# Turning the dilated queries by VectorE and DRAM instead of by TensorE, and a later place for the first pair's bias loads

## The chip, the cores and the metric

The kernel runs on one core of one Trainium2 chip. The metric is the device time of one execution in microseconds (us). Before the change it is 857.27 us, the median of three runs (856.55 to 859.91).

## The reference

Two encoder layers over 512 tokens of 1024 channels, 16 heads of 64. The first mixes tokens by dilated attention (three groups of dilation 1, 4 and 16, merged by their softmax denominators), the second by attention over a two-dimensional neighbourhood. The change lies in the first layer:

```python
def mixer_a(hn, w_in, w_out, q_gain, k_gain, t5_bias):
    proj = hn @ w_in                                  # 1024 x 10240
    qkv = proj[..., :n_qkv].reshape(b, s, 3, 3, N_HEADS, HEAD_DIM)
    gate = proj[..., n_qkv:]
    for g, (window, dilation) in enumerate(((128, 1), (512, 4), (2048, 16))):
        q = rms_norm(qkv[:, :, g, 0], q_gain[g])
        k = rms_norm(qkv[:, :, g, 1], k_gain[g])
        v = qkv[:, :, g, 2]
        reach = (window // 2) // dilation
        o, lse = dilated_group_attention(q, k, v, t5_bias[...], dilation, reach)
        ...                                           # softmax over a band, plus bias
    alpha = softmax(stack(lses)); y = sum(alpha * stack(outs))
    return (y * silu(gate)) @ w_out
```

All of it is float32. `setup_inputs` scales the gains and biases by about 8, so the precision is needed.

## The kernel before, in words

**Work and tiles.** Heads go in 8 pairs (`hc` 0 to 7). The normalised input lies as `hn_h` and `hn_l`, a high and a low part, and each weight block of 512 KB is loaded raw (`wraw`, eight slots, mostly on SyncE's queue, some added in by GpSimd's), cast by ScalarE to its high part `wh`, and its rest is made by VectorE or GpSimd as `wl`. A product is then three matmuls (high by high, low by high, high by low: the groups of three over `acc`). The products of a pair are mixed in the manner of Strassen (`mixed`), so that one pair's q, k, v and gate take 32 block jobs.

**Order.** A generator `main` emits the products and a generator `side` the attention of the pair before; `run` interleaves them by a model clock. `later_on(delay, f)` puts `f` at a later time of that clock, `yield "wait", key, delay` stays until a stamp is that old. The order so found is the program's order on TensorE (a manual schedule) and, under `held`, also on ScalarE, VectorE, GpSimd and SyncE; each engine then works its list off in that order. Nearly every operation of those engines is recorded at the line of one helper, L85; matmuls are L324, transposes on TensorE L328.

**Around the change.** When the products of a pair's queries are done, `normed("rawq")` squares, sums and scales the raw tiles (`rawq`, `rawk`: 4 row blocks of 128 tokens). `q_a` then turns tokens and channels by TensorE with an identity (`tp<-ident,rawq`, 4 transposes fill one PSUM bank): k0 and q0 of the undilated group first, then the queries of the two dilated groups, g = 0 and 1, each four transposes and one ScalarE copy into `q12` (in the profile `q<-tp`). `k_a` does the same for the dilated keys (`tp<-ident,rawk`, two groups, copied with the key gain as `k<-tp,gk`). After that `attn_a` makes the logits (`log`): per tile t two banks, one for each head, q0 by k0 as three products and then 32 small matmuls `log<-k,q` per head pair. `tp`, `log` and `o` share four PSUM banks, so the logits of tile t = 1 need the two banks that the copies of k set free.

The bias of the next pair's logits comes as six loads per pair (`e<-l_d`, `bias_a`) on SyncE's queue, the probabilities of the pair are rearranged by 16 moves `pt<-pt` there, and `weigh` multiplies them with v (`o<-pt,v`). `gt` is the gated output; `y_split` splits the outputs for the last product into `y_h` and `y_l`.

Of the kernel before, what the change touches and what calls it, by code (L numbers as in the profile page):

```python
# [13 lines left out]
F32 = mybir.dt.float32  # L14
# [8 lines left out]
P = 128  # L23
# [12 lines left out]
PB = 4  # L36
# [10 lines left out]
def tile_hybrid_encoder(  # L47
# [42 lines left out]
    @contextmanager  # L90
    def in_order():

        was, held[0] = held[0], True
        yield
        held[0] = was
# [3 lines left out]
    def sb(t, off, dims):  # L99
        return bass.AP(t.tensor, t.offset + off, [t.ap[0]] + dims)  # L100
# [54 lines left out]
    turn, pool = [0], [[2, 5]]  # L155
# [160 lines left out]
    clock = [0.0]  # L316
# [27 lines left out]
    def later_on(delay, job):  # L344

        timers.append((clock[0] + delay, job))
        timers.sort(key=lambda t: t[0])
# [92 lines left out]
    def transpose4(raw, c):  # L440
        tp = bank("tp")
        for i in range(4):
            transpose(tp[:, i * P : (i + 1) * P], raw[:, i, c : c + P])
        return tp
# [168 lines left out]
    def project_qk(n, ns, key, hc, guard, first=False, **kw):  # L613
# [22 lines left out]
            return  # L636
        normed(raw, ss, ns, key, hc)

    def normed(raw, ss, ns, key, hc):

        def go():
            with in_order() if hc == 0 and key != "raw" else nullcontext():
                head_norm(raw, ss, ns, key == "raw")
            st[key, hc] = raw
            stamp[key, hc] = clock[0]

        if (key, hc) == ("rawk", 0):
            later_on(4000, go)
        elif held[0]:
            later_on(2200, go)  # L650
        else:
            go()
# [107 lines left out]
    def q_a(hc):  # L760

        yield "wait", ("rawq", hc), (22000, 10500)[hc] if hc < 2 else 8000
        raw = st.pop(("rawq", hc))
        q0h = wk.tile([P, 512], F32R, tag="q0h", name="q0h", bufs=1)
        q0l = wk.tile([P, 512], F32R, tag="q0l", name="q0l", bufs=1)
        k0h = wk.tile([P, EXT], F32R, tag="k0h", name="k0h", bufs=1)
        k0l = wk.tile([P, EXT], F32R, tag="k0l", name="k0l", bufs=1)
        q12 = wk.tile([P, 2, 512], F32, tag="q12", name="q12", bufs=1)
        tp = bank("tp")
        for i in range(4):  # L770
            transpose(tp[:, i * P : i * P + P].rearrange("p (r j) -> p j r", j=4), raw[:, i, 3 * P :])
        act.activation(k0h[:, 64:EXT], tp, AF.Copy, scale=gk[:, 0:1])
        yield 1000
        vec.scalar_tensor_tensor(
            k0l[:, 64:EXT], tp, gk[:, 0:1], k0h[:, 64:EXT].bitcast(F32), op0=ALU.mult, op1=ALU.subtract
        )
        yield 400
        tp = transpose4(raw, 0)
        act.copy(q0h, tp)
        yield 1000  # L780
        vec.tensor_sub(q0l, tp, q0h.bitcast(F32))
        yield 400
        for g in range(2):
            act.copy(q12[:, g, :], transpose4(raw, P + P * g))
            yield
        stamp["q", hc] = 0
        st["q", hc] = q0h, q0l, q12, k0h, k0l

# [62 lines left out]
    def weighed(hc, os):  # L851
        gt, rest = st.pop(("gate", hc))
        for _ in rest:
            pass
        for j in range(4):
            g = by_class(gt)[:, :, j]
            vec.tensor_mul(g, g, os[j][:, :P].rearrange("p (t r) -> p t r", t=4))
        return gt
# [7 lines left out]
    def y_split(t, hc):  # L866
        src = t.rearrange("p (t ja x) -> p x ja t", t=4, ja=8)
        h, l = (u[:, hc, :].rearrange("p (x ja t) -> p x ja t", x=16, ja=8) for u in (st["y_h"], st["y_l"]))
        with in_order():
            act.copy(h, src)  # L870
            (vec if hc % 2 else pol).tensor_sub(l, src, h.bitcast(F32))
        stamp["ya", hc, "y"] = 0

    def bias_a(hc):
        e0 = wk.tile([P, 2, 256], F32, tag="e0", name="e0", bufs=1)
        e12 = wk.tile([P, 4, 224], F32, tag="e12", name="e12", bufs=1)
        for hd in range(2):
            h = 2 * hc + hd
            syn.dma_start(
                e0[:, hd, :],  # L880
                bass.AP(l0_d.tensor, l0_d.offset + h * 1600 + 127, [[400, 4], [-4, 32], [1, 256]]),
            )
            for g in range(2):
                syn.dma_start(
                    e12[:, 2 * hd + g, :],
                    bass.AP(l12_d.tensor, l12_d.offset + h * 512 + 256 * g + 31, [[0, 4], [-1, 32], [1, 224]]),
                )
        return e0, e12
# [49 lines left out]
    def attn_a(hc):  # L938
# [9 lines left out]
        def turn(hd, t, pr, n):  # L948

            dst = sb(pq, at(t, hd) + 256 * (4 - n), [[256, n], [1024, 4], [1, 32]])  # L950
            src = pr[:, 512 - P * n : 512]
            vec.transpose(dst, src.rearrange("p (i b k) -> p i b k", b=4, k=32))
# [12 lines left out]
        def scores(u):  # L965

            tiles = []
            for t in (2 * u, 2 * u + 1):
                cs, n = (64, 192) if t == 0 else (0, 192) if t == 3 else (0, 256)
                tiles.append((t, [bank("log") for _ in range(2)], cs, n))  # L970
            for t, lgs, cs, n in tiles:
                ks = slice(P * t + cs, P * t + cs + n)
                qs = slice(P * t, P * t + P)
                mm3_heads(
                    [lg[:, cs : cs + n] for lg in lgs],
                    lambda hs: q0h[hs, qs], lambda hs: q0l[hs, qs],
                    lambda hs: k0h[hs, ks], lambda hs: k0l[hs, ks], False,
                )
            for t, lgs, cs, n in tiles:
                for g in range(2):  # L980
                    for j in range(4):
                        c = P * t + 32 * j
                        for hd in range(2):
                            hs = slice(64 * hd, 64 * hd + 64)
                            matmul(
                                lgs[hd][32 * j : 32 * j + 32, 256 + P * g : 384 + P * g],
                                q12[hs, g, c : c + 32],
                                by_class(k12[hs, g, :])[:, :, j],
                                share=2,
                                start=False,  # L990
                                stop=(g == 1),
                            )
            return [(hd, t, lgs[hd], cs, n) for t, lgs, cs, n in tiles for hd in range(2)]
# [43 lines left out]
        def weigh():  # L1037
            os, v0 = [bank("o") for _ in range(4)], st.pop("v0")
            mms = []
            for g in range(2):  # L1040
                for b in range(4):
                    for j in range(4):
                        own = slice(32 * j, 32 * j + 32)
                        c, d = P * g, 1024 * b + 256 * (2 + g)
                        mms.append((
                            lambda hs, j=j: os[j][hs, :P],
                            lambda hs, own=own, b=b, c=c: v12[own, b, c + hs.start : c + hs.stop],
                            lambda hd, own=own, d=d: pq[own, d + at(0, hd) : d + at(0, hd) + P],
                        ))
            for i in range(4):  # L1050
                (ta, ia), (tb, ib) = ((i - 1, 1), (i, 0)) if i else ((0, 0), (3, 1))
                n, m = 32 * (tb - ta), 256 * (ib - ia) + 32 * (tb - ta)
                for a in range(4):
                    mms.append((
                        lambda hs, a=a, d=32 * ta, n=n: sb(os[a][hs], d, [[n, 2], [1, 32]]),
                        lambda hs, i=i: v0[:, i, hs],
                        lambda hd, d=run * a + 256 * ia + 32 * ta, m=m: sb(t0, d + 128 * hd, [[m, 2], [1, 32]]),
                    ))
            yield from side_by_side(mms, 4)
            return os  # L1060
# [48 lines left out]
        fill = bias_rows() if hc == 2 else None  # L1109
        yield from v_a(hc)  # L1110
        yield "wait", ("pt", hc), 2500
        st["e", hc + 1] = bias_a(hc + 1)
        yield "wait", ("pt", hc), (4500, 11500)[hc] if hc < 2 else 9000 if hc == NHC - 2 else 7500
        yield "wait", ("gate", hc), 4000
        gt = weighed(hc, (yield from weigh()))
        if hc < NHC - 2:
            send = lambda: tc.keep_in_program_order(syn.dma_start(y_d[:, hc, :], gt))
            later_on(3000, send)
            stamp["w", hc] = 0
            yield  # L1120
            if fill:
                later_on(1500, fill)
            yield 1500
            yield from q_a(hc + 1)
            return
# [391 lines left out]
```

## Time and profile before

| | |
|---|---|
| median of 3 runs | 857.27 us (856.55 to 859.91) |
| the profiled execution: own time, span | 857.42 us, 855.6 us |
| TensorE matmul busy | 833.8 us, 97% |
| VectorE, ScalarE, GpSimd busy | 636.0 us (74%), 508.8 us (59%), 294.5 us (34%) |
| mean granted clock of TensorE | 0.992 |
| moved from and to DRAM | 131.97 MB, mean 154 GB/s |

The profile records one execution. Its span lies 1.8 us below its own time, and its own time 0.15 us above the median, so a forecast made from this profile can be set against the median directly. Rows of a timeline give the start and the duration in us, the engine, the line, the operation with its tiles, the number of instructions taken together, and in brackets what an idle time before it waited for. TensorE's matmuls overlap, so that the distance between starts tells more than durations do.

### The profile page before, as it was taken

What the parts mean: (1) busy time and instruction counts of PE and PEld (TensorE: products, weight loads), DVE (VectorE), ACT (ScalarE), POOL (GpSimd) and SP (SyncE); (2) the same over time, 40 slices, a digit from 0 to 9 for tenths busy, and PEclk for the clock granted to TensorE, in tenths of its full rate; (3) what the DMA queues carried; (4) which work ended last, traced back from release to release, by engine and by line L of the source; (5) the groups of instructions that cost most, each with busy time, mean ns of one, the idle gap of its engine ahead of it and who ended that gap; (6) DMA issues with size and microseconds to landing.
All of it is one profiled execution on the core that took longest, in us unless ns stands there. A gap on an engine that the chain in (4) does not pass through costs nothing.

```text
span 855.6 us, 18127 instructions
## 1 busy us (share of the span) xinstructions
PE 833.8 (97%) x6611; PEld 689.7 (81%) x6611; DVE 636.0 (74%) x1654; ACT 508.8 (59%) x1066; POOL 294.5 (34%) x258
## 2 busy tenths in 40 slices
PE   8998989999999999999999999999999999999998
PEld 6876868878877878878878887789998898889786
DVE  7899895897897787786886865656578666776742
ACT  7566665755845846846847738545456654665440
POOL 5045442362453543443533512113123322322301
PEclk9999999999999999999999999999999999999999
DMA  9425755776576775776776554283264456534212
GB/s 339 137 59 136 205 130 140 135 176 189 133 183 191 156 189 168 162 174 180 152 181 179 117 184 142 75 300 113 80 193 142 124 170 183 162 131 127 84 50 99
DMA packets 56169, 131.97 MB, mean 154 GB/s; under 512 B 7184, under 2 KB 24528, under 8 KB 55952
## 3 DMA queue, kind: packets, MB, share of 16 engines
q1 hardware_dynamic: 49744, 108.78, 40.9%
q0 software_dynamic: 6048, 22.02, 15.3%
q8 instruction: 52, 0.85, 0.4%
q14 instruction: 37, 0.30, 0.1%
q10 hardware_dynamic: 288, 0.01, 0.0%
HBM read 111.73 MB, written 11.72 MB: 144 GB/s over the span
## 4 chain that ended last, share of the span: by engine, by line
PE 74%; DVE 9%; ACT 8%; DMA 4%; issue 3%; SPq 1%; POOL 1%; DVEq 0%; ACTq 0%
PE acc L324 61%; ACT p L85 5%; PE o L324 4%; PE log L324 4%; PE tp L328 3%; DMA wraw<-in_w 2%; DVE wl L85 2%; SPq L85 1%; ACT rawk L85 1%; ACT wh L85 1%; DVE na L85 1%; DVE rawq L85 1%; DVE p L85 1%; DVE gt L85 1%; DMA pt<-in_xt 1%
## 5 line engine op out<-in xcount | busy, mean ns | idle before, releaser
L85 POOL TENSOR_TENSOR wl<-wraw,wh 128x512 fp32r<-128x512 f32 (+1 forms) x153 | 197.6, 1292 | 426.8 <-PE acc L324 227.8
L85 ACT CAST wh<-wraw 128x512 fp32r<-128x512 f32 (+1 forms) x360 | 209.4, 593 | 196.6 <-PE acc L324 160.1
L85 DVE TENSOR_TENSOR wl<-wraw,wh 128x512 fp32r<-128x512 f32 (+1 forms) x207 | 160.2, 777 | 43.2 <-PE acc L324 34.3
L324 PE MATMUL acc<-wh,hn_h 128*128 128x384 f32 (+1 forms) x488 | 185.9, 381 | 2.9 <-DVE gt L85 1.7
L324 PE MATMUL acc<-wl,hn_h 128*128 128x384 f32 (+1 forms) x488 | 176.7, 362 | 1.4 <-DVE wl L85 1.4
L324 PE MATMUL acc<-wh,hn_l 128*128 128x384 f32 (+1 forms) x488 | 176.8, 362 | 0.0
L85 ACT ACTIVATE p<-p,mn 128x256 f32<-128x256 f32 (+2 forms) x248 | 137.5, 583 | 32.3 <-DVE mn L85 32.3
L324 PEld LDWEIGHTS acc<-wh,hn_h 128*128 128x128 f32 x488 | 91.8, 188 | 21.4 <-issue 6.8
L324 PEld LDWEIGHTS acc<-wl,hn_h 128*128 128x128 f32 x488 | 91.9, 188 | 9.8 <-DVE wl L85 2.5
L324 PEld LDWEIGHTS acc<-wh,hn_l 128*128 128x128 f32 x488 | 91.6, 188 | 9.6
L324 PE MATMUL acc<-wl,mix_h 128*128 128x512 f32 x224 | 87.9, 393 | 2.1 <-DVE wl L85 2.1
L324 PE MATMUL acc<-wh,mix_h 128*128 128x512 f32 x224 | 89.5, 400 | 0.0
L324 PE MATMUL acc<-wh,mix_l 128*128 128x512 f32 x224 | 87.8, 392 | 0.0
L324 PE MATMUL acc<-hn_h,wh 128*128 128x512 f32 x192 | 79.0, 411 | 0.3 <-ACT rawb L85 0.2
L324 PE MATMUL acc<-hn_h,wl 128*128 128x512 f32 x192 | 75.2, 391 | 0.0
L324 PE MATMUL acc<-hn_l,wh 128*128 128x512 f32 x192 | 74.9, 390 | 0.0
L85 DVE STREAM_TRANSPOSE pt<-p 128x512 f32<-128x512 f32 (+1 forms) x60 | 40.6, 687 | 23.7 <-ACT p L85 23.5
L85 DVE TENSOR_REDUCE ss<-sq 128x4 f32<-128x256 f32 (+1 forms) x96 | 46.1, 501 | 11.9 <-POOL sq L85 6.2
L324 PE MATMUL acc<-y_h,wh 128*128 128x512 f32 x128 | 52.3, 409 | 0.0
L324 PEld LDWEIGHTS acc<-wl,mix_h 128*128 128x128 f32 x224 | 42.4, 189 | 11.5 <-DVE wl L85 3.3
L324 PE MATMUL acc<-y_h,wl 128*128 128x512 f32 x128 | 50.5, 394 | 0.0
L324 PE MATMUL acc<-y_l,wh 128*128 128x512 f32 x128 | 50.4, 394 | 0.0
(149 smaller groups left out, 1373.0 us busy)
## 6 DMA issues: line engine op xcount, KB each, us to landing
wraw<-in_w SPq DMA_DIRECT2D x95, 512.0 KB
wraw<-in_w POOLq DMA_DIRECT2D x42, 512.0 KB, 6.9
wraw<-in_w SPq DMA_DIRECT2D x38, 384.0 KB
pt<-pt SPq DMA_DIRECT2D x112, 64.0 KB
td<-tr SPq DMA_DIRECT2D x24, 224.0 KB
pt<-td SPq DMA_DIRECT2D x24, 224.0 KB
e<-l_d SPq DMA_DIRECT2D x32, 112.0 KB
e<-l_d SPq DMA_DIRECT2D x16, 128.0 KB
```

The source lines that it names most:

```text
L85: m = f(*args, **kw)
L324: nc.tensor.matmul(o, l, r, **kw)
L328: nc.tensor.transpose(o, i, ident)
```

## The change

There are four parts.

1. For pairs 2 to 7 a new function `move_q` takes the dilated queries off TensorE. As soon as a pair's `rawq` blocks are scaled, VectorE turns them in 32x32 blocks (four instructions `qt<-rawq`), ScalarE's queue writes them to DRAM in two transfers (`qd<-qt`, 256 KB each) and reads them back in four (`q<-qd`, 128 KB each, in runs of 512 bytes). `q_a` then leaves out 8 transposes and 2 copies per pair and waits in the model clock for the last read.
2. `q12` has another order of columns. Pairs 0 and 1 keep TensorE's transposes but need four half copies where two whole ones were.
3. The rest `y_l` of pair 1 is made by GpSimd instead of VectorE.
4. `bias_a(1)`, the loads of the bias for the second pair, is emitted behind the first pair's `weigh` instead of ahead of it.

```diff
+    def move_q(raw, hc):
+        d = dr.tile([2, P, 512], F32, tag="qd", name="qd", bufs=2)
+        halves = []
+        def turn(i):
+            if i % 2 == 0:
+                halves.append(wk.tile([P, 512], F32, tag="p", name="qt", bufs=PB))
+            dst = sb(halves[-1], 32 * (i % 2), [[64, 2], [128, 4], [1, 32]])
+            vec.transpose(dst, raw[:, i, P : 3 * P].rearrange("p (g b k) -> p g b k", g=2, k=32))
+            if i % 2:
+                later_on(1500, partial(act.dma_start, d[i // 2], halves[-1]))
+        def read(b):
+            if b == 0:
+                st["q12", hc] = wk.tile([P, 1024], F32, tag="q12", name="q12", bufs=1)
+            dst = sb(st["q12", hc][32 * b : 32 * b + 32], 0, [[128, 8], [1, 128]])
+            src = bass.AP(d.tensor, d.offset + 128 * b, [[512, 32], [512 * 32, 8], [1, 128]])
+            act.dma_start(dst, src)
+            if b == 3:
+                stamp["q12", hc] = clock[0]
+        for i in range(4):
+            later_on(1600 + 1000 * i, partial(turn, i))
+            later_on(11500 + 800 * i, partial(read, i))
...
         def go():
+            if key == "rawq" and hc > 1:
+                move_q(raw, hc)
...
-        for g in range(2):
-            act.copy(q12[:, g, :], transpose4(raw, P + P * g))
+        for g in range(0 if moved else 2):
+            tp = transpose4(raw, P + P * g).rearrange("p (h t j r) -> p h t j r", h=2, t=2, j=4)
+            for h in range(2):
+                act.copy(sb(q12, 512 * h + 64 * g, [[32, 2], [128, 4], [1, 32]]), tp[:, h])
             yield
+        if moved:
+            yield "wait", ("q12", hc), 0
+            q12 = st.pop(("q12", hc))
...
-            (vec if hc % 2 else pol).tensor_sub(l, src, h.bitcast(F32))
+            (vec if hc % 2 and hc > 1 else pol).tensor_sub(l, src, h.bitcast(F32))
...
-                        c = P * t + 32 * j
+                        c = 512 * (t // 2) + 128 * j + 64 * g + 32 * (t % 2)
...
-        st["e", hc + 1] = bias_a(hc + 1)
+        if hc:
+            st["e", hc + 1] = bias_a(hc + 1)
         yield "wait", ("pt", hc), (4500, 11500)[hc] if hc < 2 else 9000 if hc == NHC - 2 else 7500
         yield "wait", ("gate", hc), 4000
         gt = weighed(hc, (yield from weigh()))
+        if not hc:
+            st["e", hc + 1] = bias_a(hc + 1)
```

What the change does to the lists of the engines is shown at three places. On ScalarE before the change, in pair 4, from the cast of q0 to the two copies of the dilated keys (the `wh` behind q0h is the cast of v's first weight block):

```order
263 L85 CAST q0h<-tp 128x512
264 L85 CAST wh<-wraw 128x512
265 L85 COPY q_3949<-tp 128x512 x2
266 L85 ACTIVATE gt<-acc 128x512
267 L85 ACTIVATE eg<-gt 128x512
268 L85 CAST wh<-wraw 128x512
269 L85 ACTIVATE k_4030<-tp,gk 128x512
270 L85 CAST wh<-wraw 128x512
271 L85 ACTIVATE k_4030<-tp,gk 128x512
```

and the same place after it:

```order
270 L85 CAST q0h<-tp 128x512
271 L85 DMA q_3994<-qd 32x8x128 x2
272 L85 CAST wh<-wraw 128x512
273 L85 DMA q_3994<-qd 32x8x128 x2
274 L85 ACTIVATE k_4022<-tp,gk 128x512
275 L85 ACTIVATE gt<-acc 128x512
276 L85 ACTIVATE eg<-gt 128x512
277 L85 CAST wh<-wraw 128x512
278 L85 ACTIVATE k_4022<-tp,gk 128x512
```

The two copies of q are gone, and the issues of four reads stand around the cast of v's block, ahead of both copies of k. The two writes `qd<-qt` stand a few rows further up.

On VectorE after the change, in pair 4, where the queries are scaled; the four rows `qt<-rawq` are new:

```order
510 L85 TENSOR_TENSOR rawq<-rawq,rs 128x512
511 L85 TENSOR_TENSOR wl<-wraw,wh 128x512
512 L85 STREAM_TRANSPOSE qt<-rawq 128x2x4x32
513 L85 TENSOR_TENSOR rawq<-rawq,rs 128x512
514 L85 TENSOR_TENSOR rawk<-rawk,acc 128x512
515 L85 STREAM_TRANSPOSE qt<-rawq 128x2x4x32
516 L85 TENSOR_TENSOR rawq<-rawq,rs 128x512
517 L85 TENSOR_TENSOR rawk<-rawk,acc 128x512
518 L85 STREAM_TRANSPOSE qt<-rawq 128x2x4x32
519 L85 TENSOR_TENSOR rawq<-rawq,rs 128x512
520 L85 TENSOR_TENSOR wl<-wraw,wh 128x512
521 L85 STREAM_TRANSPOSE qt<-rawq 128x2x4x32
```

So the turns go between steps that were there before, and everything behind them on VectorE moves back by their time.

On SyncE in the first pair, before (-) and after (+): the moves of the probabilities, the six bias loads and the weight load next to them.

```order
-L85 DMA pt_874<-pt 32x512 x16
-L85 DMA e_1306<-l_d 128x1x256
-L85 DMA e_1307<-l_d 128x1x224 x2
-L85 DMA e_1306<-l_d 128x1x256
-L85 DMA e_1307<-l_d 128x1x224 x2
-L85 DMA wraw<-in_w 128x1024
+L85 DMA pt_876<-pt 32x512 x16
+L85 DMA wraw<-in_w 128x1024
+L85 DMA e_1483<-l_d 128x1x256
+L85 DMA e_1484<-l_d 128x1x224 x2
+L85 DMA e_1483<-l_d 128x1x256
+L85 DMA e_1484<-l_d 128x1x224 x2
```

One weight load has changed places with the six bias loads. TensorE's list in pairs 0 and 1 is what it was; in pairs 2 to 7 the two groups of four transposes of `rawq` are gone, and in pairs 3 to 6 three products that stood ahead of the logits stand behind those of the first two tiles, so that the logits come that much sooner.

More of the change, by code (lines that the diff above doesn't have):

```diff
@@ L767, in q_a @@
         k0l = wk.tile([P, EXT], F32R, tag="k0l", name="k0l", bufs=1)
-        q12 = wk.tile([P, 2, 512], F32, tag="q12", name="q12", bufs=1)
+        moved = hc > 1
+        q12 = None if moved else wk.tile([P, 1024], F32, tag="q12", name="q12", bufs=1)
         tp = bank("tp")
@@ L986, in scores @@
                                 lgs[hd][32 * j : 32 * j + 32, 256 + P * g : 384 + P * g],
-                                q12[hs, g, c : c + 32],
+                                q12[hs, c : c + 32],
                                 by_class(k12[hs, g, :])[:, :, j],
```

## The prediction

> **What bounds the kernel now.** I read the page first: its head, the busy times and the DMA queues.
>
> ```profile
> span 855.6 us, 18127 instructions
> PE 833.8 (97%) x6611; PEld 689.7 (81%) x6611; DVE 636.0 (74%) x1654; ACT 508.8 (59%) x1066; POOL 294.5 (34%) x258
> q1 hardware_dynamic: 49744, 108.78, 40.9%
> ```
>
> TensorE is busy 97% of the span. So TensorE work taken away is worth its full time, if nothing else is late where it goes; and the 3% of waits are what other engines can still make worse. The timeline of TensorE at pair 2's queries prices a group of four transposes.
>
> ```profile
> 203.14 0.60 PE L328 MATMUL tp<-ident,rawq 128*128 128x128 f32 x4
> 203.50 0.47 PE L324 MATMUL acc<-wh,hn_h 128*128 128x512 f32 x1
> 203.81 0.39 PE L324 MATMUL acc<-wl,hn_h 128*128 128x512 f32 x1
> 204.04 0.39 PE L324 MATMUL acc<-wh,hn_l 128*128 128x512 f32 x1
> ```
>
> A product goes every 0.23 us (203.81 to 204.04). From 203.14 to 204.04 are 0.90 us, with the group and two products in them: 0.90 - 2 x 0.23 = 0.44 us for the group. Two groups per pair are 0.88 us.
>
> Then I followed the waits to see what is late where the queries are turned. ScalarE's timeline in pairs 2 to 6, at the cast of v's first weight block and at the second copy of k (of pair 4 more of the chain):
>
> ```profile
> 202.92 0.62 ACT L85 CAST wh<-wraw 128x512 fp32r<-128x512 f32 x1 [3.49 <-DMA wraw<-in_w]
> 209.30 0.69 ACT L85 ACTIVATE k<-tp,gk 128x512 f32<-128x512 f32 x1
> 266.64 0.62 ACT L85 CAST wh<-wraw 128x512 fp32r<-128x512 f32 x1 [5.40 <-DMA wraw<-in_w]
> 270.91 0.68 ACT L85 ACTIVATE k<-tp,gk 128x512 f32<-128x512 f32 x1
> 327.91 0.62 ACT L85 CAST wh<-wraw 128x512 fp32r<-128x512 f32 x1 [3.17 <-DMA wraw<-in_w]
> 328.43 1.06 ACT L85 COPY q<-tp 128x512 f32<-128x512 f32 x2
> 329.39 0.61 ACT L85 ACTIVATE gt<-acc 128x512 f32<-128x512 f32 x1
> 332.17 0.69 ACT L85 ACTIVATE k<-tp,gk 128x512 f32<-128x512 f32 x1
> 389.51 0.62 ACT L85 CAST wh<-wraw 128x512 fp32r<-128x512 f32 x1 [2.62 <-DMA wraw<-in_w]
> 394.30 0.69 ACT L85 ACTIVATE k<-tp,gk 128x512 f32<-128x512 f32 x1
> 451.81 0.62 ACT L85 CAST wh<-wraw 128x512 fp32r<-128x512 f32 x1 [2.80 <-DMA wraw<-in_w]
> 456.41 0.69 ACT L85 ACTIVATE k<-tp,gk 128x512 f32<-128x512 f32 x1
> ```
>
> In every pair ScalarE stands 2.6 to 5.4 us for v's weights, and all that must be done before the logits is queued behind that wait. TensorE's rows at the second tile of the logits, which needs the banks that the copies of k set free:
>
> ```profile
> 210.95 0.30 PE L324 MATMUL log<-k0h,q0h 64*128 64x256 f32 x2
> 271.64 0.38 PE L324 MATMUL log<-k0h,q0h 64*128 64x256 f32 x1 [0.71 <-ACT k L85]
> 333.83 0.30 PE L324 MATMUL log<-k0h,q0h 64*128 64x256 f32 x2
> 396.00 0.30 PE L324 MATMUL log<-k0h,q0h 64*128 64x256 f32 x2
> 458.11 0.30 PE L324 MATMUL log<-k0h,q0h 64*128 64x256 f32 x2
> ```
>
> The copy of k ends 332.17 + 0.69 = 332.86 in pair 4, 394.99 in pair 5, 457.10 in pair 6: about 1.0 us ahead of the logits. In pair 3 there is no room, and TensorE waits 0.71. So behind the 97% stands a chain with a microsecond of slack: v's weights, ScalarE, logits. Why the weights are late is in SyncE's rows and the sums of a window before pair 4's wait ends (columns: length; busy of PE, PEld, DVE, ACT, POOL; clock, DMA share, GB/s).
>
> ```profile
> 306.56 4.97 SPq L85 DMA_DIRECT2D e<-l_d  x6
> 311.69 7.59 SPq L85 DMA_DIRECT2D wraw<-in_w  x3
> 318.00:328.00 10.00, 10.00 (x52) 8.23 (x51) 8.08 (x25) 4.17 (x8) 2.62 (x2) 1.00 0.85 256
> ```
>
> The three loads are issued from 311.69, behind the bias loads, ScalarE gets the first of its block at 327.91, and the DMA engines are 85% busy meanwhile: this wait is one for transfers.
>
> **The change part by part.** *TensorE.* Pairs 2 to 6 lose 5 x 0.88 = 4.4 us. Pair 7's 0.88 falls into a wait that is there already (1.89 us, quoted below) and counts nothing. The logits also come sooner against the rest: by 0.88 and by one triple of products that now stands behind them (0.69), 1.57 us in pairs 3 to 6, and by 0.88 and four triples, 3.64 us, in pair 2.
>
> *Transfers.* Per pair 512 KB are written and read back by the same engines that bring v's weights. q1's mean packet, 108.78 MB / 49744 = 2.2 KB, is of the size of the writes' (2 KB) and takes 0.409 x 16 x 855.6 / 49744 = 113 ns; for small ones there is a window of 2 us around 253 us, full of packets under 2 KB:
>
> ```profile
> q1 hardware_dynamic: 201, 0.20, 30.1%
> ```
>
> 0.301 x 16 x 2 us / 201 = 48 ns each. The writes are 256 packets, 16 per engine: 1.8 us. The reads are 1024, 64 per engine: 3.1 us, half of them issued before the cast that waits for v. What v's weights come later, d, is therefore 0 to 1.8 + 1.5 = 3.3 us: 0 if all of it fits into the gaps, 3.3 if none does. Of the 10 us window 15%, 1.5 us, is free: I take 3.3 - 1.5 = 1.8. Here the Trainium skill ("DMA: Bandwidth & Descriptors", Issuing engines are not separate DMA queues) speaks against the change: transfers started by ScalarE interleave on the same 16 engines, and another queue saves only issue time. By that rule d is above 0; with a queue of its own it would be 0 and the sum 14 us lower; no row of this trace has bulk traffic on ScalarE's queue.
>
> *ScalarE.* Behind the cast the copies of q go (328.43 to 329.39, 0.96), and one cast (327.91 to 328.43, 0.52) no longer stands ahead of the second copy of k; two DMA issues come. One takes at most 4.97 / 6 = 0.83 us by SyncE's row above, and I take 0.5, 1.0 for two. From the wait's end to the end of k it was 4.95 us in pair 4; it becomes 4.95 - 0.96 - 0.52 + 1.0 = 4.5. In pair 2, where more stands between, 7.07 becomes 5.5 by the same steps with one cast and issue more. The new wait of the logits for the second tile is then:
> pair 2: 202.92 + 5.5 + d - (210.95 - 3.64) = 1.1 + d;
> pair 3: 266.64 + 4.5 + d - (270.93 - 1.57) = 1.8 + d, less the 0.71 it had, 1.1 + d;
> pair 4: 327.91 + 4.5 + d - (333.83 - 1.57) = 0.15 + d;
> pair 5: d - 0.4; pair 6: d - 0.2.
> With d = 1.8 these are 2.9, 2.9, 1.95, 1.4 and 1.6, together 10.75 us.
>
> *The clock.* What follows a wait of this size is read from windows of 3.4 us.
>
> ```profile
> 125.80:129.20 3.40, 0.63 (x10) 0.51 (x10) 3.02 (x12) 0.55 (x2) 1.33 (x2) 1.00 0.96 199
> 129.20:132.60 3.40, 3.40 (x57) 3.28 (x58) 2.08 (x7) 0.00 (x0) 0.00 (x0) 0.50 0.26 78
> 514.90:518.30 3.40, 1.51 (x9) 0.99 (x8) 3.40 (x8) 3.37 (x8) 1.31 (x1) 1.00 0.90 323
> 518.30:521.70 3.40, 3.40 (x12) 2.72 (x11) 1.93 (x5) 2.98 (x6) 0.00 (x0) 0.50 0.76 294
> 269.00:272.40 3.40, 2.65 (x33) 1.68 (x39) 3.40 (x5) 3.10 (x6) 1.65 (x1) 1.00 0.33 126
> ```
>
> After windows with 0.63 and 1.51 us of TensorE work the granted clock is 0.50 for 3.4 us, a loss of 1.7 us; the wait of 0.71, in a window with 2.65 of work, was followed by none. So the bound lies between 0.75 and 1.89 us idle in one window. At 0.75 all five new waits cost a half clock (8.5 us); at 1.89 only the longer ones, when they fall well, two of them (3.4). I take the middle, 6.0. The Trainium skill ("TensorE: Matmul & The Clock Gate", Part 1) has the clock fall to half only after at least one idle window of about 3.4 us; by it none of these waits would cost anything more. The rows disagree, as 1.51 us of work stood in the window before a half clock. It is a rival below.
>
> *VectorE* gets 4 turns per pair. The list of groups by form has turns of the same 256 columns:
>
> ```profile
> L85 DVE STREAM_TRANSPOSE pt<-p 128x256 f32<-128x256 f32 x4 | 1.7, 425 | 0.0
> ```
>
> 4 x 0.425 = 1.7 us per pair. What hides them is VectorE's idle 26%: I take 0, and 1.7 x 6 = 10 if they all fell where TensorE waits for its rests `wl`. The two more half copies of pairs 0 and 1 lie on ScalarE, which is 59% busy: 0, at most 4 x 0.6 = 2.4.
>
> *The rest of pair 1 and the first bias loads.* At pair 7, in order of the engines:
>
> ```profile
> 513.27 0.61 ACT L85 CAST wh<-wraw 128x512 fp32r<-128x512 f32 x1
> 513.40 1.51 DVE L85 TENSOR_TENSOR y_l<-yr,y_h 128x512 fp32r<-128x512 f32 x1 [1.84 <-ACT y_h L85]
> 514.81 0.69 DVE L85 TENSOR_TENSOR wl<-wraw,wh 128x512 fp32r<-128x512 f32 x1
> 517.22 0.66 PE L328 MATMUL tp<-ident,rawk 128*128 128x128 f32 x4 [1.89 <-DVE k0l L85]
> ```
>
> Without the `y_l` the next step, `wl`, can go when its cast ends, 513.88: 0.9 us sooner, and so can TensorE, which waits behind it. -0.9, between 0 (GpSimd's `y_l` late instead) and -3.6 (the whole wait and its half clock). In the first pair TensorE waits where the bias loads are:
>
> ```profile
> 124.53 6.13 SPq L85 DMA_DIRECT2D e<-l_d  x6
> 128.08 0.58 PE L324 MATMUL o<-pt,v 128*64 128x64 f32 x8 [2.90 <-DMA e<-l_d]
> ```
>
> The product needs the moved probabilities, which go ahead of the bias in the same queue, so the name `e<-l_d` is the last one in that queue and not what is needed. With the bias behind, the moves still have to land. I take 0; if the bias packets held them up, it is up to -(2.9 + 1.7) = -4.6, the wait and the half clock behind it.
>
> **The sum.** 857.4 - 4.4 + 10.75 + 6.0 - 0.9 = 868.9, say 869 us. The profiled execution (857.42) is at the median (857.27), so nothing is corrected.
>
> **The rivals.**
> Faster: a shorter ScalarE. The transfers fit into the gaps (d = 0) and ScalarE's issues cost next to nothing, so that the chain from v's weights to the second k falls to 3.5 us in pairs 3 to 6 and 4.5 in pair 2; then the new waits are 0.1 and 0.1 and the saving carries through: 857.4 - 4.4 + 0.2 - 0.9 = 852.3, and with the first pair's stall gone too 847.7. It decides where d and two issues together are under 0.4 us. For it: a mean load of the DMA engines by q1 of 41%, and two copies off ScalarE. Against it: 85% in the very window, and the 1.57 us by which the logits come sooner.
> The same: d = 0, with issues of 0.5 us. The waits are 1.1 + 1.1 + 0.15 = 2.3, too short for the clock: 857.4 - 4.4 + 2.3 - 0.9 = 854.4.
> The clock keeps full speed: as forecast without the 6.0, 863.
> Worse: d = 3.3, or the last reads land so late that the logits of q wait for them: waits 10.75 + 5 x 1.5 = 18.3 and 8.5 of clock: 857.4 - 4.4 + 18.3 + 8.5 - 0.9 = 879. It decides where the first weights of v come over 3 us later than TensorE's steps around them.
>
> **How the numbers follow.** A measurement of this kernel can tell about 0.5%, 4.3 us, from no change: faster is below 853.1, slower above 861.7. Forecast (a wait at the logits, 864 to 875) 0.39; clock rule 0.10; worse 0.09; same 0.13; faster 0.29, of it 0.12 with the first pair's stall gone. So faster 0.29, same 0.13, slower 0.58. The range reaches from 849, which leaves out about half of the 847.7 case, to 880, which leaves out the upper half of the worst: 849 to 880.
>
> **What would show it.** Right: 0.88 us less of `tp<-ident,rawq` in each of pairs 2 to 7; v's casts on ScalarE with longer waits (4 to 7 us); new waits of `log` for ScalarE's k of 1 to 3 us in pairs 2 to 6; half clock after most of them. Wrong: `log` without such waits and shorter pairs (then the transfers cost nothing), or waits of `log` for `q<-qd` itself (then it is the way through DRAM that is long, not the sharing), or the wait at 128 us gone (then the bias packets did hold up the moves), or VectorE's `wl` as what TensorE waits for.

## The result, and the profile after

The changed kernel takes 884.18 us (median of four runs, 881.43 to 887.44), the kernel before beside it 857.37 us: a ratio of 1.0312, with a 95% interval of 1.0273 to 1.0351. The forecast was 869 us with a range of 849 to 880. The direction was right, the size was not: 27 us instead of 12. The profiled execution took 881.43 us. Ratios leave out executions in the kernel's slower state; among the runs below that is one, of the kernel with only the reads cut.

From the page: the head, the busy times, the new traffic on ScalarE's queue (packets, MB, share of 16 engines) and the chain that ended last; then TensorE's waits (us in total, times, longest).

```profile
span 879.7 us, 18119 instructions
PE 841.1 (96%) x6563; PEld 692.7 (79%) x6563; DVE 632.4 (72%) x1677; ACT 503.5 (57%) x1058; POOL 294.6 (33%) x259
q10 hardware_dynamic: 8544, 6.31, 2.7%
PE 60%; DMA 13%; DVE 12%; ACT 8%; issue 3%; SPq 3%; POOL 1%; ACTq 0%; DVEq 0%; POOLq 0%
```

```profile
PE log L324 <- ACT k L85: 15.7, 9, 3.0
PE o L324 <- DMA e<-l_d: 3.0, 1, 3.0
PE log L324 <- DMA q<-qd: 2.7, 3, 1.5
```

The 48 transposes of pairs 2 to 7 are gone (6611 matmuls to 6563), and yet TensorE is busy 7 us longer. The waits at the logits have grown from 0.7 to 18.4 us. Two windows show where the loss lies. A pair's stage starts with the product that waits 0.19 us for `rawq`; the first window goes from the start of pair 2 to that of pair 7, the second holds pair 4 alone (length; busy of PE, PEld, DVE, ACT, POOL; clock, DMA share, GB/s). Before the change:

```profile
180.12:492.12 312.00, 310.29 (x2941) 250.40 (x2941) 254.19 (x634) 203.37 (x396) 134.42 (x110) 1.00 0.69 168
305.72:367.84 62.12, 61.92 (x589) 50.03 (x589) 50.52 (x127) 40.67 (x80) 26.32 (x22) 1.00 0.69 169
```

After it:

```profile
181.31:518.87 337.56, 319.78 (x2901) 255.48 (x2901) 249.78 (x654) 198.90 (x386) 132.52 (x110) 0.96 0.69 171
316.94:385.21 68.27, 64.32 (x580) 51.52 (x581) 49.68 (x131) 39.96 (x78) 26.52 (x22) 0.95 0.71 170
```

These five pairs hold 25.6 us more, the whole loss; the rest of the kernel is 1.5 us shorter. TensorE's idle time rose from 1.7 to 17.8 us, by 16.1. Its busy time rose by 9.5 although 4.4 to 4.6 us of work are gone, so the same products took about 14 us longer. The granted clock accounts for that: after the change eight windows of 3.41 us in these pairs have a clock of 0.50 (one each in pairs 2 and 5, two each in pairs 3, 4 and 6), before it none. They last 27.3 us, and half of that, 13.65 us, is lost. Per pair that is about 3.2 us of new waits and 2.7 us of slow clock.

ScalarE's timeline in pair 4, the pair with the longest issues, shows where the waits come from.

```profile
335.36 0.59 ACT L85 CAST q0h<-tp 128x512 fp32r<-128x512 f32 x1 [0.71 <-PE tp L328]
339.52 1.27 ACTq L85 DMA_DIRECT2D q<-qd  x2
341.19 0.62 ACT L85 CAST wh<-wraw 128x512 fp32r<-128x512 f32 x1 [5.24 <-PE acc L324]
341.74 2.99 ACTq L85 DMA_DIRECT2D q<-qd  x2
344.77 0.69 ACT L85 ACTIVATE k<-tp,gk 128x512 f32<-128x512 f32 x1 [2.97 <-DMA q<-qd]
345.36 0.59 ACT L85 ACTIVATE gt<-acc 128x512 f32<-128x512 f32 x1
345.98 0.63 ACT L85 ACTIVATE eg<-gt 128x512 f32<-128x512 f32 x1
346.52 0.60 ACT L85 CAST wh<-wraw 128x512 fp32r<-128x512 f32 x1
347.02 0.68 ACT L85 ACTIVATE k<-tp,gk 128x512 f32<-128x512 f32 x1
```

The last two reads take 2.99 us to be issued, and ScalarE, which issues them, stands 2.97 us before the copy of k. In pairs 3, 5 and 6 the same two take 1.57, 1.86 and 1.58 us. TensorE at the same place, in SyncE's rows just above it the loads that the pair waits for:

```profile
317.98 4.92 SPq L85 DMA_DIRECT2D e<-l_d  x6
323.07 9.43 SPq L85 DMA_DIRECT2D wraw<-in_w  x3
345.51 0.38 PE L324 MATMUL log<-k0h,q0h 64*128 64x256 f32 x1 [1.89 <-ACT k L85]
347.76 0.58 PE L324 MATMUL log<-k0h,q0h 64*128 64x256 f32 x1 [1.86 <-ACT k L85]
```

The semaphore events of the trace say what an issue stands for. Transfers of SyncE's and ScalarE's queues use eight completion semaphores in turn, and the four reads went out at 339.52, 340.47, 341.74 and 344.42, each 0.02 to 0.09 us after the last increment from the transfer that had used its semaphore before: a bias load issued at 321.73 and three weight loads issued at 323.07, 331.68 and 332.18. So a read that is to be issued by ScalarE waits until an older load of SyncE's queue has landed, and everything on ScalarE waits with it; this is called its stand below. In the trace the read's own instruction, or the one just ahead of it, names that semaphore as what it waits for. So the stand comes from how this program hands out its semaphores; that the queue itself would hold the read back is not shown.

### The profile page after: what moved, and what is told of

It is laid out like the page before. It is cut to its first block, busy times and chain, and to the rows that moved or that the text cites. A ratio compares the mean times of both kernels' runs of the same rounds, so it can differ in the third digit from the quotient of the medians.

```text
span 879.7 us, 18119 instructions
## 1 busy us (share of the span) xinstructions
PE 841.1 (96%) x6563; PEld 692.7 (79%) x6563; DVE 632.4 (72%) x1677; ACT 503.5 (57%) x1058; POOL 294.6 (33%) x259
## 4 chain that ended last, share of the span: by engine, by line
PE 60%; DMA 13%; DVE 12%; ACT 8%; issue 3%; SPq 3%; POOL 1%; ACTq 0%; DVEq 0%; POOLq 0%
PE acc L324 50%; DMA wraw<-in_w 6%; PE log L324 5%; ACT p L85 4%; DVE wl L85 3%; DMA e<-l_d 3%; SPq L85 3%; PE o L324 2%; DMA q<-qd 2%; PE tp L328 2%; DVE na L85 2%; DVE rawq L85 1%; ACT wh L85 1%; DVE ss L85 1%; DMA gb_d<-rp 1%
## 5 line engine op out<-in xcount | busy, mean ns | idle before, releaser
L85 DVE TENSOR_TENSOR wl<-wraw,wh 128x512 fp32r<-128x512 f32 (+1 forms) x207 | 154.8, 750 | 53.5 <-PE acc L324 45.0
L324 PE MATMUL acc<-wh,hn_h 128*128 128x384 f32 (+1 forms) x488 | 187.9, 385 | 2.8 <-DVE gt L85 1.7
L324 PE MATMUL acc<-wl,hn_h 128*128 128x384 f32 (+1 forms) x488 | 178.9, 367 | 1.8 <-DVE wl L85 1.8
```

Source lines behind the costliest of these rows:

```text
L85: m = f(*args, **kw)
L324: nc.tensor.matmul(o, l, r, **kw)
```

## The experiments

Two causes were to be told apart: ScalarE's stand for the issue of the reads (theory A) and the bytes of the queries, which delay the weights (theory B, the forecast's own).

**Bytes gone, issues kept.** Writes cut to 16 columns, reads to 32 rows of 64 bytes, on the same queue at the same places:

```diff
-                later_on(1500, partial(act.dma_start, d[i // 2], halves[-1]))
+                later_on(1500, partial(act.dma_start, d[i // 2][:, :16], halves[-1][:, :16]))
...
+                pol.memset(st["q12", hc][:, 16:], 0.01)
-            dst = sb(st["q12", hc][32 * b : 32 * b + 32], 0, [[128, 8], [1, 128]])
-            src = bass.AP(d.tensor, d.offset + 128 * b, [[512, 32], [512 * 32, 8], [1, 128]])
+            dst = sb(st["q12", hc][32 * b : 32 * b + 32], 0, [[1, 16]])
+            src = bass.AP(d.tensor, d.offset, [[512, 32], [1, 16]])
```

> The changed kernel with its six transfers of q per pair kept at their places but cut to 8 KB (writes) and 2 KB (reads); the rest of q12 is filled by GpSimd with a constant, so the dilated logits are left out of the computation. Theory A (the issue waits): each transfer on ScalarE's or SyncE's queue may only be issued when the transfer eight issues before it has landed, whichever queue that one was in; the reads' predecessors are bias and weight loads, and ScalarE stands there with all behind it. The waits do not depend on the size of the reads, so the time stays near the changed kernel's, 868 to 882. Theory B (the forecast: q's bytes delay v's weights): the bytes are gone, so 852 to 858.

Measured: 857.74 us, ratio 1.0007 (0.998 to 1.0034). By these words theory A has fallen: a stand whose length does not depend on the bytes is not what costs 27 us, and theory B's range is met. But the stand is still there, only shorter, as ScalarE's rows of pair 4 show:

```profile
332.12 1.52 ACTq L85 DMA_DIRECT2D q<-qd  x2
333.68 0.69 ACT L85 ACTIVATE k<-tp,gk 128x512 f32<-128x512 f32 x1 [1.54 <-PE acc L324]
```

The issues of the last two reads take 1.52 us instead of 2.99: the loads that they wait for land sooner.

**Bytes kept, issues off ScalarE.** The four reads on SyncE's queue, and in another kernel on GpSimd's:

```diff
-            act.dma_start(dst, src)
+            syn.dma_start(dst, src)      # in the other kernel: pol.dma_start(dst, src)
```

> The changed kernel with the four reads of q issued by SyncE instead of ScalarE; all bytes stay. Theory A: ScalarE is free, but SyncE stands at the same waits with the next weight loads behind it, 855 to 870. Theory B: 874 to 886.

> The changed kernel with the four reads of q issued by GpSimd instead of ScalarE; all bytes stay. Theory A: ScalarE no longer stands for the issue of reads, the waits of the logits for k go, 852 to 864; GpSimd then stands for the writes to land, and its wl may be late. Theory B: the bytes still delay the weights, 874 to 886.

Measured: on SyncE's queue 864.13 us, ratio 1.0095 (1.0067 to 1.0122); on GpSimd's 882.62 us, 1.0297 (1.0235 to 1.0359). The first is what theory A said: with all bytes there, about 19 of the 27 us go when ScalarE is free. Its ScalarE rows, and its pair 4 as a window:

```profile
336.88 0.62 ACT L85 CAST wh<-wraw 128x512 fp32r<-128x512 f32 x1 [4.10 <-DMA wraw<-in_w]
337.40 0.68 ACT L85 ACTIVATE k<-tp,gk 128x512 f32<-128x512 f32 x1
339.65 0.68 ACT L85 ACTIVATE k<-tp,gk 128x512 f32<-128x512 f32 x1
```

```profile
313.76:376.23 62.47, 61.62 (x581) 49.59 (x581) 50.50 (x131) 39.85 (x78) 26.72 (x22) 1.00 0.74 185
```

The cast stands 23.1 us behind the pair's start (336.88 - 313.76), against 22.2 before (327.91 - 305.72) and 24.25 after (341.19 - 316.94). By the semaphore events the weights themselves landed 0.1 us ahead of the cast before the change and here, so that they are 0.9 us late here; after the change they landed at 340.45, 1.4 us late, and the cast came 0.7 us behind them, as the second read was issued in between. From the cast to the end of the second k it is 3.45 us here, against 6.5 after. What is left of the loss in this kernel are waits at the logits for q (5.6 us) and for k (2.9), and three windows of half clock.

The second kernel has theory B's time, but its waits are those of neither theory. The waits for k fell from 15.7 to 2.9 us, as with the reads on SyncE's queue, so it was the stand that made them. In their place TensorE waits for q itself,

```profile
PE log L324 <- DMA q<-qd: 15.2, 9, 2.8
```

and in pair 4 a read lands a median of 7.5 us after its issue (count, KB each, us to landing):

```profile
q<-qd POOLq DMA_DIRECT2D x4, 128.0 KB, 7.5
```

Slow reads are not GpSimd's alone. By the semaphore events the median over all pairs is 7.1 us in this kernel, 6.4 for ScalarE's reads in the changed kernel and 4.8 for SyncE's in the kernel above. So q is late in the changed kernel too, hidden behind the waits for k. On SyncE's queue the reads go out ahead of the next two weight loads, in pair 4 of the changed kernel behind them; whether this order or the issuing engine makes them quicker was not tried apart.

**Neither.** The small transfers again, the reads on SyncE's queue:

> As the first of these runs (all transfers of q cut to 8 and 2 KB, constant queries), with the reads issued by SyncE. No bytes and no stand of ScalarE: the saving on TensorE should come through as far as it can, 850 to 856 if ScalarE's stand cost anything in that first run (857.74), 857 to 858 if it cost nothing there.

Measured: 849.35 us, ratio 0.9919 (0.9892 to 0.9946). Pair 4 takes what TensorE's work takes:

```profile
302.07:363.27 61.20, 61.01 (x581) 49.26 (x581) 49.53 (x131) 39.97 (x78) 27.64 (x23) 1.00 0.71 172
```

61.20 us instead of 62.12, 0.92 less. The four kernels make a table, as ratios to the kernel before:

| | reads issued by ScalarE | by SyncE |
|---|---|---|
| all bytes | 1.031 | 1.0095 |
| 8 KB and 2 KB | 1.0007 | 0.992 |

The bytes cost 1.8% without ScalarE's stand, the stand 0.9% without the bytes; together they cost 3.9%, more than the sum. The stand passes the lateness of any old load on to ScalarE, and the bytes make those loads late. Part of the excess is clock: pairs 2 to 6 have eight windows of half clock in the changed kernel, but two with the bytes cut, three with the reads on SyncE's queue, and none with both.

**Which bytes.** Only the writes cut (the reads take their 128 KB from the weights in DRAM), and only the reads cut:

> The changed kernel with whole reads but writes cut to 8 KB; the reads take their 128 KB each from the weights in DRAM, so the dilated queries are left out of the computation. By the runs so far the bytes and ScalarE's stand for issues act together. Theory W (the writes' bytes, issued ahead of v's weights, make the weights land late, and ScalarE stands for them): 857 to 864. Theory R (the reads' bytes do it, 1024 short packets per pair): 870 to 884.

> The changed kernel with whole writes but reads cut to 2 KB, the rest of q12 filled by GpSimd with a constant, so the dilated queries are left out. Theory W: 870 to 884, as the writes are still ahead of v's weights. Theory R: 856 to 863.

Measured: writes cut 874.22 us, ratio 1.0215 (1.019 to 1.024); reads cut 870.81 us, ratio 1.0142 (1.0079 to 1.0204), its runs spread from 860.6 to 876.0. Neither theory is right alone: of the 3.1% the reads alone keep 2.15%, the writes alone 1.4%. The first of these kernels differs in one more thing, as its reads do not have to wait for the writes. A finer split the spread does not allow.

**The bias loads out of SyncE's queue.** In all these kernels six bias loads go out right ahead of v's weights. Issued by GpSimd instead, in the changed kernel and in the kernel before:

```diff
     def bias_a(hc):
-            syn.dma_start(
+            pol.dma_start(
...
-                syn.dma_start(
+                pol.dma_start(
```

> The changed kernel with the six bias loads of each pair issued by GpSimd instead of SyncE. If the bias loads in SyncE's queue ahead of v's weights are what makes those weights late, so that ScalarE's stand is long: weights earlier, 855 to 868. If the weights are late for the total of bytes: 878 to 886. Rival: GpSimd's issue makes its wl late, above 886.

> The kernel before with the six bias loads of each pair issued by GpSimd: the control for the last run (855.93). If the bias loads only hurt where ScalarE stands for transfers, little changes, 854 to 858 (pair 3's wait of 0.7 for k goes). If they cost the kernel before as well, 848 to 853, and then the moved queries bring nothing even with the bias out of the way.

Measured: changed kernel 855.93 us, ratio 0.9995 (0.9971 to 1.0019); kernel before 862.25 us, 1.0082 (1.0055 to 1.0109). SyncE's and ScalarE's rows of the changed kernel with this edit, in pair 4:

```profile
308.63 3.60 SPq L85 DMA_DIRECT2D wraw<-in_w  x4
326.60 0.88 ACTq L85 DMA_DIRECT2D q<-qd  x2
327.85 0.62 ACT L85 CAST wh<-wraw 128x512 fp32r<-128x512 f32 x1 [1.45 <-PE acc L324]
327.88 2.07 ACTq L85 DMA_DIRECT2D q<-qd  x2
330.37 0.69 ACT L85 ACTIVATE k<-tp,gk 128x512 f32<-128x512 f32 x1 [1.90 <-PE tp L328]
```

Four weight loads are issued in 3.60 us where three took 9.43 (of which the first alone took 8.45), and k's copy now waits for TensorE's transposes and not for an issue. All bytes are there, ScalarE issues the reads as in the change, and the whole loss of 3.1% is gone: so the backlog behind the bias loads is what made the loads late enough for the stand to hurt. The Trainium skill ("DMA: Bandwidth & Descriptors", Why a DMA increments its semaphore by 16 and not by 1) has a transfer use the largest number of engines, up to 16, that divides the slowest dimension of both of its sides; for the bias loads, whose source has a slowest dimension of 4, that would be 4 of 16. The trace agrees: each of the 48 bias loads on SyncE's queue shows five increments of its semaphore, one right after its issue and four at its landing, where every weight load shows sixteen.

The first weight load behind the bias loads, which holds v's first block, lands in two parts. In pair 4 before the change twelve of its increments had come by 322.90 and the last four came from 326.36 to 327.81, close behind the four of the last bias load (325.08 to 326.71). After the change the twelfth came at 336.25, the last four from 339.06 to 340.45, and those of the last bias load from 337.79 to 339.43. With the bias loads issued by GpSimd the two weight loads issued at 308.63 and 309.34 have no such gap: 0.1 and 0.7 us from the twelfth increment to the next. That fits a quarter of v's block waiting behind the bias loads on the four engines that both use. No view names the engines, and bias loads of another shape at the same place were not tried.

In the kernel before the same edit costs 6.5 us, against the expectation, which had no loss in it. TensorE waits for other things there, in the first pairs above all:

```profile
PE o L324 <- DMA pt<-pt: 5.4, 3, 4.0
PE o L324 <- issue: 2.8, 2, 1.9
```

The waits at the first pair's products were 3.4 us and are 5.4, and a 6.8 us half clock follows instead of 3.4.

**The rest of the change alone**, parts 3 and 4 on the kernel before:

```diff
-            (vec if hc % 2 else pol).tensor_sub(l, src, h.bitcast(F32))
+            (vec if hc % 2 and hc > 1 else pol).tensor_sub(l, src, h.bitcast(F32))
...
-        st["e", hc + 1] = bias_a(hc + 1)
+        if hc:
+            st["e", hc + 1] = bias_a(hc + 1)
...
+        if not hc:
+            st["e", hc + 1] = bias_a(hc + 1)
```

> The kernel before with only parts 3 and 4 of the change: pair 1's y_l on GpSimd, the bias loads of the second pair behind the first pair's products. Both theories: 0 to 1 us faster (856.3 to 857.4), the wait of 2.9 us at the first pair's products with v stays, since it is for the moved probabilities. Rival: the bias packets did hold up the moves, then 852 to 854.

Measured: 856.95 us, ratio 1.0 (0.9973 to 1.0026). The wait of the first pair is still there:

```profile
128.22 0.57 PE L324 MATMUL o<-pt,v 128*64 128x64 f32 x8 [2.92 <-DMA e<-l_d]
```

So it was not for the bias, although the row names it: by the semaphore events it ended as a move landed at 128.13, and the bias loads landed from 132.0 on. With the bias loads on GpSimd's queue, in the changed kernel, the same wait is put down to the moves:

```profile
PE o L324 <- DMA pt<-pt: 3.4, 2, 2.9
```

The 0.9 us expected of part 3 is too little for this run to show.

**Versions that beat both.** Bias loads by GpSimd and reads by SyncE; then pair 1's bias loads back on SyncE's queue; then pair 2's too:

```diff
-            act.dma_start(dst, src)
+            syn.dma_start(dst, src)
...
-            syn.dma_start(                       # in bias_a, twice
+            pol.dma_start(                       # next: (pol if hc > 1 else syn), then hc > 2
```

> The changed kernel with the bias loads issued by GpSimd and the reads of q by SyncE: both causes undone with all bytes there. If the two causes are all: TensorE's saving comes through, 849 to 853, the lowest of all with the right result. If the bytes still cost by themselves: 855 to 860. Rival: SyncE stands for the writes to land with the next weights behind, and TensorE waits for q: above 860.

> The changed kernel with the reads of q on SyncE's queue, and the bias loads on GpSimd's queue for pairs 2 to 7 only; pair 1's stay on SyncE's. In the last run the first pair's waits were 4.3 us with 6.8 us of half clock after them, against 3.4 us of half clock in the kernel before: with pair 1's bias back on SyncE's queue 849 to 852 if GpSimd's issues made those waits; 852 to 854, no change, if they did not.

> As the run before it, with pair 2's bias loads on SyncE's queue too. The wait of 1.7 us at pair 2 for VectorE's gt should go if GpSimd's issues made it; v's weights of pair 2 then come late again behind the bias, with a half clock of 1.7 us: 850 to 855, about the same as the run before it.

Measured: 852.88 us, ratio 0.996 (0.9939 to 0.9981); 850.94 us, 0.9941 (0.9919 to 0.9962); 851.9 us, 0.996 (0.9941 to 0.9979). All three are faster than before, with all work done; the second is the lowest, though the three intervals overlap. Against the kernel before with the same bias edit (1.0082) the moved queries and the rest of the change gain 1.2% in the first of them, more than the 0.5% that TensorE's saving is worth; the difference was not taken apart.

## Why the prediction was wrong in size

**TensorE's saving** was right: 0.88 us a pair forecast, 0.92 seen where nothing else is late (61.20 against 62.12).

**The transfers.** The forecast took d, the lateness of v's weights, as 1.8 us out of 0 to 3.3. In pair 4 they landed 1.4 us later with the reads on ScalarE, and 0.9 with the reads on SyncE's queue. The step was sound. The bytes were priced a little high: 1.8 + 3.1 = 4.9 us per engine and pair, against at most 0.027 x 879.7 / 6 = 4.0 by q10, which holds some other packets too.

**ScalarE: the step that failed first.** "One takes at most 4.97 / 6 = 0.83 us by SyncE's row above, and I take 0.5, 1.0 for two." That row holds bias loads whose semaphores were free when their turn came. In pair 4 the two reads behind the cast took 2.99 us, and from the cast to the end of the second k it was 347.70 - 341.19 = 6.5 us instead of 4.5. Over pairs 2 to 6 the timelines give 6.8, 4.6, 6.5, 6.2 and 5.4 us where the forecast had 5.5 and four times 4.5: 29.5 instead of 23.5. Of the 5.35 us that the waits had too little, 2.0 are for q in pairs 5 and 6; the longer way to k covers the rest. (In pair 2 the 5.5 does not follow from the steps named, which give 7.07 - 0.96 - 1.04 + 1.5 = 6.6.)

The prediction showed one row in which issues are slow: three weight loads of SyncE's, 7.59 us. It is another delay. By the instruction records the first of the three took 6.55 us by itself, with its semaphore free since 307.27, and the other two under 0.4 each. The row could have warned that an issue has no small fixed price; the stand of the reads it does not show. The forecast did not ask what the issue of a read has to wait for, nor what that does to an engine that also computes.

**The waits** were forecast as one per pair, 10.75 us in all. All five pairs have two. In pairs 2 to 4 both are for k, as the second tile's two banks come free one by one, each with its own copy of k: 3.02 and 0.71 us in pair 2, 1.89 and 1.86 in pair 4. In pairs 5 and 6 one is for q (0.5 and 1.5), which the forecast had named as a sign against itself. The list of ScalarE after the change has `gt`, `eg` and a cast between the two copies of k, where one cast stood before; the forecast followed the second copy alone. New waits in pairs 2 to 6: 16.1 us.

**The clock: the larger miss.** It was forecast at 6.0, with at most one half-clock window of 3.4 us behind each wait. Pair 4 in windows of 3.4 us:

```profile
339.87:343.28 3.41, 3.41 (x21) 2.56 (x21) 1.44 (x2) 0.62 (x1) 0.00 (x0) 1.00 1.08 304
343.28:346.69 3.41, 0.72 (x7) 0.35 (x5) 0.43 (x2) 1.88 (x4) 0.00 (x0) 1.00 0.57 148
346.69:350.10 3.41, 2.34 (x53) 2.02 (x58) 2.24 (x4) 2.04 (x4) 1.34 (x1) 0.50 0.08 25
350.10:353.52 3.42, 3.42 (x37) 2.54 (x22) 2.71 (x15) 0.00 (x0) 0.01 (x1) 0.50 0.00 0
353.52:356.93 3.41, 3.41 (x16) 2.79 (x15) 1.61 (x6) 2.99 (x7) 2.10 (x2) 1.00 0.30 64
```

The first wait and the start of the second leave 0.72 us of work in one window, and the next has the half clock. The rest of the second wait lies in that one (2.34 us of work), and the clock stays at half for another. So five pairs have eight such windows and the term is 13.65 us. The sum by these numbers: 857.4 - 4.4 + 16.1 + 13.65 - 1.5 = 881.25, close to the profiled execution's 881.43. (The -1.5 is the rest of the kernel, which the forecast had at -0.9.) The rival by which these waits cost no clock has fallen: as in the rows of before, the window ahead of the half clock held work (0.72 us), where the Trainium skill ("TensorE: Matmul & The Clock Gate", Part 1) asks for an idle one.

What was right is the way it goes: weights late, ScalarE behind them, logits waiting for k, half clock behind the waits.

**The other terms.** The first pair's wait stayed, as forecast (3.0 us, and 2.9 before), but the half clock behind it lasted 6.8 us instead of 3.4. So the -1.5 of the rest of the kernel is 1.2 us more ahead of pair 2 and 2.7 less from pair 7 on. VectorE's turns, priced at 0.425 us each, show as

```profile
L85 DVE STREAM_TRANSPOSE qt<-rawq 128x256 f32<-128x256 f32 x24 | 10.3, 431 | 0.0
```

and no wait of TensorE names them. At pair 7 TensorE's wait of 1.89 for `k0l` is gone, as forecast, but two waits at the logits came in its place:

```profile
545.92 0.38 PE L324 MATMUL log<-k0h,q0h 64*128 64x256 f32 x1 [1.12 <-ACT k L85]
547.45 1.50 PE L324 MATMUL log<-k,q 64*32 64x128 f32 x62 [0.58 <-DMA q<-qd]
```

**The range** ended at 880 because its worst case had one half clock for each of five waits, 8.5 us. Its waits, 18.3 us, were more than the 16.1 that came, though for other reasons: a later v or later reads, not the issues. With 13.65 in place of 8.5 that case alone would have reached 884.

## What to carry to other kernels

Before transfers are put on the queue of an engine that computes, ask what their issue may have to wait for. Here it was an older transfer on either of two queues that shared their completion semaphores, with the whole engine behind it. The price of an issue that goes freely is no bound for one that has to wait; which semaphore an issue waits for, and when the transfer before it on that semaphore lands, can be read from the trace. And price two short waits close together as one slow stretch: here the second fell into the half clock of the first and prolonged it.

## What the runs showed of the hardware that was not expected

The issue of a transfer on ScalarE's queue followed the landing of an older load of SyncE's queue within 0.1 us, four times out of four in pair 4. Bytes and stand together cost 3.9%, while 1.8% and 0.9% were measured for each alone. A weight load behind six bias loads on the same queue landed in two parts, the last four of its sixteen increments from 3.5 us behind the twelfth on (pair 4 before the change). A read of 128 KB landed a median of 6.4 us after its issue by ScalarE, and 7.1 by GpSimd, beside the weight loads. Two waits of 1.9 us, 0.4 us apart, brought 6.8 us of half clock.
